# A hybrid attention and state-space block on one core: attention emitted in small pieces at fixed places, one softmax scaling moved into the head's norm, group norm one unit later

## Chip, cores, metric

One core of one Trainium2 chip. The metric is the device time of one execution, in microseconds (us). The kernel before takes 1214.12 us (median of three runs, 1212.49 to 1216.79).

## What is computed

One decoder block over 512 positions of width 1024, in float32:

```python
h = rms_norm(x, norm_mix_g);  proj = h @ w_in          # q, k, v, z, xbc, dt, gates
a = softmax(q1 k1 + bias) - lam * softmax(q2 k2 + bias)  # causal, 8 heads, two maps of 64 each
o = rms_norm(a @ v, attn_subln_g) * (1 - lam_init)      # per head, 128 wide
xbc = silu(causal_dwconv(xbc));  y = ssd_chunked_scan(...)   # 4 groups of 8 heads, chunks of 128
y = group rms_norm((y + xs * d_skip) * silu(z))
mixed = sigmoid(g_attn) * (y_attn @ w_proj_attn) + sigmoid(g_ssm) * (y_ssm @ w_proj_ssm)
x = x + mixed @ w_out
u = causal_dwconv(rms_norm(x) @ w_up);  x = x + (silu(u_gate) * u_val) @ w_down
```

## The kernel before

Every large product is made of three matmuls: each operand is split into a high part and a low remainder (xH, xL; weights wh, wl), and high*high, high*low and low*high are summed in PSUM. A c-tile (ctile) is 24 such matmuls of 512 columns for 128 output channels; a token block (in_block, L214) is four times 24 matmuls of 256 columns. Weights come in 179 units of 128x1024. `Weights.load` issues the DMA, casts to the high part on ScalarE (L83) and subtracts for the low part on VectorE or, for the numbers in `pool_units` (L75), on GpSimd (L86). Three raw buffers and four pairs of parts are kept, and a load is given a priority 600 instructions ahead of its place.

The program runs in this order:

- The norm of x, then dt and its cumulative sums, whose transposes (L267) go to TensorE.
- The state-space stage: 64 units in the hand-written order SSD_UNITS, each a convolved c-tile (B, C, x), a gate c-tile (z, e) or an output projection (p). `at` hangs steps of the chunked scan, and the transposes tokens_b and tokens_x (L325), behind unit numbers. SSD_AT gives for each group the units after which its chunks, its statistics (chunk_stat) and its group_norm are emitted. group_norm starts with the matmuls L483 that need the diagonal tile made by ScalarE at L474.
- Attention: for each of four head pairs att_in makes q, k and v in three token blocks and norms q and k. att_prep transposes them for one head, att_head runs four row blocks: logits (L654, L655), bias and row maximum on VectorE, exponentials on ScalarE, the second map scaled on ScalarE (L663), the difference on VectorE (L664). A queue `pending` holds each block's transposes (L610) back by AVLAG = 2 blocks and its products with v (L620) by one more; the fourth ends in the head's norm (L629 to L636) and finish (L642 to L646).
- Mix: per c-tile a gate c-tile, then the c-tile with yaH and yaL (the head outputs), then m, mH, mL.
- The output projection, the second norm, the feed-forward part.

The framework turns the emitted program into one queue for each engine. Emission order is the priority, and where its plan finds an instruction not ready in time, a later one goes ahead. So the matmuls of the next in_block lie partly between those of att_head. [...]

PSUM holds three c-tile accumulators (mm), two for transposes (tpp) and, in attention, two for logits (lgp) and one for the head's output (pop).

## Time and profile before

| | |
|---|---|
| median of three runs | 1214.12 us |
| the profiled execution | 1212.06 us |
| its span, first to last instruction | 1209.9 us |
| TensorE busy / VectorE / ScalarE / GpSimd | 1144.9 / 775.8 / 594.2 / 237.4 us |
| mean granted TensorE clock | 0.977 |

PE is the matmul engine, PEld its weight loads, DVE VectorE, ACT ScalarE, POOL GpSimd, SP SyncE with the DMA queue. L204 is line 204 of the kernel. [...] The matmul records overlap, so the pace of matmuls is read from counts over stretches and not from the length of one record.

### The profile page before, as it was taken

The page shows a single profiled execution, that of the slowest core. Times are in us where ns is not written, and L with a number is a line of the kernel's source. Part 1 is how long each engine was busy: PE and PEld are TensorE (multiplying, and loading weights), DVE is VectorE, ACT ScalarE, POOL GpSimd, SP SyncE. Part 2 cuts the span into 40 slices and gives each one's busy share as a digit, 9 for nine tenths or more (in the row PEclk, how much of TensorE's full clock was granted, in tenths as well). Part 3 has the DMA queues.
Part 4 walks back from the last instruction along what each step waited for, and adds up shares of the span by engine and source line. Part 5 has one row for each costly group of instructions (what it writes and reads, how often), then busy time and mean ns, then how long its engine had stood idle before and what let it go on. Part 6 is the DMA issues. An engine that isn't in the chain of part 4 may idle for free.

```text
span 1209.9 us, 15891 instructions
## 1 busy us (share of the span) xinstructions
PE 1144.9 (95%) x5934; PEld 960.8 (79%) x5934; DVE 775.8 (64%) x1312; ACT 594.2 (49%) x1154; POOL 237.4 (20%) x206
## 2 busy tenths in 40 slices
PE   5899997999999999998988988999999999999998
PEld 4688776887887889997978766887888888888887
DVE  7767768679876565468585875444777777773221
ACT  5674665665574232558484873233444444441210
POOL 2024334333433320451423000003000000000000
PEclk9899998999999999999898998999999999999999
DMA  6552332342433223221212112244232323323330
GB/s 221 91 134 93 119 100 80 124 118 90 133 109 96 70 87 117 72 75 44 71 42 73 53 36 70 90 136 135 75 105 90 102 90 103 101 92 115 112 105 18
DMA packets 56125, 114.47 MB, mean 95 GB/s; under 512 B 20640, under 2 KB 28496, under 8 KB 56048
## 3 DMA queue, kind: packets, MB, share of 16 engines
q1 hardware_dynamic: 56048, 113.45, 30.4%
q8 instruction: 47, 0.77, 0.3%
q14 instruction: 30, 0.25, 0.1%
HBM read 111.19 MB, written 2.24 MB: 94 GB/s over the span
## 4 chain that ended last, share of the span: by engine, by line
PE 78%; DVE 9%; ACT 8%; issue 3%; POOL 1%; DMA 1%; SPq 0%; POOLq 0%; ACTq 0%; DVEq 0%
PE mm L204 20%; PE mm L205 20%; PE mm L206 20%; PE mm L222 3%; PE mm L224 3%; PE mm L223 3%; DVE xc L318 1%; ACT wh L83 1%; DVE Bc L318 1%; PE sm L452 1%; PE po L620 1%; PE lg L654 1%; ACT dec L401 1%; ACT p L659 1%; PE sm L429 1%
## 5 line engine op out<-in xcount | busy, mean ns | idle before, releaser
L83 ACT CAST wh<-wr 128x1024 fp32r<-128x1024 f32 x179 | 187.4, 1048 | 253.0 <-PE mm L205 224.8
L86 DVE TENSOR_TENSOR wl<-wr,wh 128x1024 fp32r<-128x1024 f32 x130 | 160.2, 1233 | 101.9 <-ACT wh L83 100.6
L204 PE MATMUL mm<-xH,wh 128*128 128x512 f32 x456 | 184.1, 404 | 7.3 <-ACT xH L175 7.1
L206 PE MATMUL mm<-xH,wl 128*128 128x512 f32 x456 | 180.2, 395 | 0.7 <-DVE wl L86 0.7
L205 PE MATMUL mm<-xL,wh 128*128 128x512 f32 x456 | 180.2, 395 | 0.0
L86 POOL TENSOR_TENSOR wl<-wr,wh 128x1024 fp32r<-128x1024 f32 x49 | 118.4, 2426 | 151.5 <-ACT wh L83 125.4
L206 PE MATMUL mm<-hH,wl 128*128 128x512 f32 x352 | 137.7, 391 | 0.0
L204 PE MATMUL mm<-hH,wh 128*128 128x512 f32 x352 | 137.6, 391 | 0.0
L205 PE MATMUL mm<-hL,wh 128*128 128x512 f32 x352 | 137.6, 391 | 0.0
L222 PE MATMUL mm<-wh,xH 128*128 128x256 f32 x384 | 111.9, 291 | 5.1 <-ACT qksq L532 5.1
L223 PE MATMUL mm<-wl,xH 128*128 128x256 f32 x384 | 111.1, 289 | 0.0
L224 PE MATMUL mm<-wh,xL 128*128 128x256 f32 x384 | 110.7, 288 | 0.0
L204 PEld LDWEIGHTS mm<-xH,wh 128*128 128x128 f32 x456 | 86.9, 191 | 25.8 <-ACT xH L175 7.1
L206 PEld LDWEIGHTS mm<-xH,wl 128*128 128x128 f32 x456 | 86.6, 190 | 19.1 <-DVE wl L86 1.1
L205 PEld LDWEIGHTS mm<-xL,wh 128*128 128x128 f32 x456 | 86.8, 190 | 17.8 <-DVE xL L176 0.5
L222 PEld LDWEIGHTS mm<-wh,xH 128*128 128x128 f32 x384 | 75.8, 197 | 5.8 <-ACT qksq L532 5.7
L204 PEld LDWEIGHTS mm<-hH,wh 128*128 128x128 f32 x352 | 66.4, 189 | 13.9
L205 PEld LDWEIGHTS mm<-hL,wh 128*128 128x128 f32 x352 | 66.4, 189 | 13.9
L206 PEld LDWEIGHTS mm<-hH,wl 128*128 128x128 f32 x352 | 66.4, 189 | 13.7
L318 DVE SCALAR_TENSOR_TENSOR xc<-raw,pc,xc 128x512 f32<-128x512 f32 x48 | 64.9, 1353 | 18.9 <-ACT xc L316 18.1
L223 PEld LDWEIGHTS mm<-wl,xH 128*128 128x128 f32 x384 | 75.8, 197 | 0.2
L224 PEld LDWEIGHTS mm<-wh,xL 128*128 128x128 f32 x384 | 75.8, 197 | 0.1
(229 smaller groups left out, 2240.6 us busy)
## 6 DMA issues: line engine op xcount, KB each, us to landing
wr<-in_ws SPq DMA_DIRECT2D x179, 512.0 KB, 3.5
dec<-cum_d SPq DMA_DIRECT2D x16, 512.0 KB, 4.4
ec<-ecum_d SPq DMA_DIRECT2D x24, 128.0 KB, 3.7
...
```

The lines of the kernel that those rows point to most:

```text
L83: nc.scalar.copy(out=hi, in_=raw)
L86: eng.tensor_sub(out=lo, in0=raw, in1=hi.bitcast(F32))
L204: T.matmul(ps, lhsT=h, rhs=rH(k), start=(k == 0), stop=False)
L205: T.matmul(ps, lhsT=h, rhs=rL(k), start=False, stop=False)
L206: T.matmul(ps, lhsT=l, rhs=rH(k), start=False, stop=(k == n - 1))
L222: T.matmul(ps, lhsT=xH[k][:, sl], rhs=h, start=(k == 0), stop=False)
L223: T.matmul(ps, lhsT=xH[k][:, sl], rhs=l, start=False, stop=False)
L224: T.matmul(ps, lhsT=xL[k][:, sl], rhs=h, start=False, stop=(k == NK - 1))
L318: V.scalar_tensor_tensor(out=dst, in0=raw[:, j:j + S], scalar=w[j], in1=dst, op0=ALU.mult, op1=ALU.add)
L401: A.activation(out=dec[:, h], in_=dec[:, h], func=AF.Relu, scale=-1.0, bias=qcol[:, 0, c, g * HPG + h:g * HPG + h + 1])
L429: T.matmul(yo[:, j * P:(j + 1) * P], lhsT=state[:, j * P:(j + 1) * P], rhs=st["C"][:, cs], start=True, stop=True)
L452: T.matmul(yd[(h % 2) * 64:(h % 2) * 64 + 64, (h // 2) * P:(h // 2 + 1) * P], lhsT=xk[:, h * 64:(h + 1) * 64], rhs=dec[:, h], start=True, ...
```

## The change

- Attention is emitted piece by piece. block_pieces cuts a token block into eight pieces of 12 matmuls, gate_pieces a gate c-tile into four of 6, pa_pieces the first 7/8 of an attention projection into four. Lists give, for each head, the piece after which prep, logits, flip_a, values and head_out stand. A pair's steps lie between the pieces of the next pair and of one gate c-tile. The last pair's lie between five gate c-tiles and three unfinished attention projections. `pending`, `late` and AVLAG are gone; the eight gates have tiles of their own (gts).
- Softmax: the block is left scaled by its first map's sum. One small coefficient cf replaces the ScalarE pass L663, and the scale r is applied in the head's norm. For the first two row blocks both maps share one PSUM tile, one bias addition and one maximum.
- The norm of q and k is one chain of 32 columns in place of two of 16.
- group_norm of groups 0 to 2 stands one unit later; z1 stands ahead of p0, and x3 ahead of p3, in groups 2 and 3; the first tokens_b stands two units later and the first tokens_x one.
- The low parts of the 31 odd units 3 to 63 are made on VectorE in place of GpSimd; GpSimd makes those of units 71 to 90 (before: 71 to 88), among which there are now two gate units.
- The tile cb comes from another pool, rsqrt has other buffer counts, and an unused column is no longer computed.

```diff
-        o += [(n, g - 2 if n[0] == "p" else g) for n in "B z0 C p0 x0 p1 x1 p2 x2 p3 x3 z1 z2 z3".split()]
+        o += [(n, g - 2 if n[0] == "p" else g) for n in "B z0 C z1 p0 x0 p1 x1 p2 x2 x3 p3 z2 z3".split()]
...
-SSD_AT = [(11, (12, 14, 16, 18), (12, 15, 17, 19), 21, 22),
-          (22, (23, 25, 28, 31), (23, 26, 29, 32), 34, 35),
-          (35, (36, 38, 41, 44), (36, 39, 42, 45), 47, 48),
+SSD_AT = [(11, (12, 14, 16, 18), (12, 15, 17, 19), 21, 23),
+          (22, (23, 25, 28, 31), (23, 26, 29, 32), 34, 36),
+          (35, (36, 38, 41, 44), (36, 39, 42, 45), 47, 49),
           (47, (48, 50, 52, 54), (48, 51, 53, 55), 57, 58)]
...
-        self.pool_units = frozenset(range(3, 65, 2)) | frozenset(range(71, 89))
+        self.pool_units = frozenset(range(71, 91))
...
-        it = small.tile([P, 16], I32, name="rsi", bufs=3)[:, :n]
-        y = small.tile([P, 16], F32, name="rsy", bufs=3)[:, :n]
-        t = small.tile([P, 16], F32, name="rst", bufs=2)[:, :n]
+        it = small.tile([P, 32], I32, name="rsi", bufs=2)[:, :n]
+        y = small.tile([P, 32], F32, name="rsy", bufs=2)[:, :n]
+        t = small.tile([P, 32], F32, name="rst", bufs=4)[:, :n]
...
+            at.setdefault(n + (2 if n else 4), []).append(lambda: tokens_b(st))
...
-            at.setdefault(n + 2, []).append(lambda: tokens_x(g, j, xc))
+            at.setdefault(n + (3 if n < 4 else 2), []).append(lambda: tokens_x(g, j, xc))
...
-    def att_in():
-        st = {}
-        for nm in ("q", "k"):
-            raw = ap.tile([P, 4, 4, 64], F32, name="qk", bufs=4)
-            ss = small.tile([P, 16], F32, name="qkss", bufs=2)
-
-            def done(t, ps):
-                A.copy(out=raw[:, t].rearrange("p a d -> p (a d)"), in_=ps)
...
-            in_block(done)
-            v = small.tile([P, 16], F32, name="qkv", bufs=2)
-            V.tensor_scalar(out=v, in0=ss, scalar1=1.0 / 64, scalar2=1e-6, op0=ALU.mult, op1=ALU.add)
-            rr = small.tile([P, 16], F32, name="qkr", bufs=2)
-            rsqrt(v, rr, 16)
...
+    pairs = [{} for _ in range(4)]
...
+    def block_pieces(done):
+
+        u, hold = [], {}
+
+        def piece(t, half):
+            if not u:
+                u.extend(W.next() for _ in range(2))
+            if half == 0:
+                hold["ps"] = mm.tile([P, S], F32, name="mm")[:, :256]
+            ps = hold["ps"]
+            sl = slice(t * P, (t + 1) * P)
+            for k in range(4 * half, 4 * half + 4):
+                h, l = (w[:, (k % 4) * 256:(k % 4 + 1) * 256] for w in u[k // 4])
+                T.matmul(ps, lhsT=xH[k][:, sl], rhs=h, start=(k == 0), stop=False)
+                T.matmul(ps, lhsT=xH[k][:, sl], rhs=l, start=False, stop=False)
+                T.matmul(ps, lhsT=xL[k][:, sl], rhs=h, start=False, stop=(k == NK - 1))
+            if half == 1:
+                done(t, ps)
+        return [lambda t=t, half=half: piece(t, half) for t in range(4) for half in range(2)]
...
+    def gate_pieces(c):
...
+        def piece(i):
+            if i == 0:
+                hold["w"], hold["ps"] = W.next(), mm.tile([P, S], F32, name="mm")
+            (h, l), ps = hold["w"], hold["ps"]
+            for k in range(2 * i, 2 * i + 2):
+                hk, lk = h[:, k * P:(k + 1) * P], l[:, k * P:(k + 1) * P]
+                T.matmul(ps, lhsT=hk, rhs=xH[k], start=(k == 0), stop=False)
+                T.matmul(ps, lhsT=hk, rhs=xL[k], start=False, stop=False)
+                T.matmul(ps, lhsT=lk, rhs=xH[k], start=False, stop=(k == NK - 1))
+            if i == 3:
+                V.tensor_mul(out=gts[c], in0=ps, in1=r_bc)
+                A.activation(out=gts[c], in_=gts[c], func=AF.Tanh, scale=0.5)
...
+    def pair_pieces(p_):
...
+            A.copy(out=raw[:, t].rearrange("p a d -> p (a d)"), in_=ps)
+            sq = ap.tile([P, 4, 64], F32, name="qksq", bufs=1)
+            A.activation(out=sq.rearrange("p a d -> p (a d)"), in_=ps, func=AF.Square, scale=r_col[:, t:t + 1])
+            V.tensor_reduce(out=ss[:, i * 16 + t * 4:i * 16 + (t + 1) * 4], in_=sq, axis=AX.X, op=ALU.add)
+            if i == 1 and t == 3:
+                v = small.tile([P, 32], F32, name="qkv", bufs=2)
+                V.tensor_scalar(out=v, in0=ss, scalar1=1.0 / 64, scalar2=1e-6, op0=ALU.mult, op1=ALU.add)
+                rr = small.tile([P, 32], F32, name="qkr", bufs=2)
+                rsqrt(v, rr, 32)
+                for j, nm in enumerate("qk"):
+                    r1 = rr[:, j * 16:(j + 1) * 16]
+                    V.tensor_mul(out=r1.rearrange("p (t a) -> p t a", t=4), in0=r1.rearrange("p (t a) -> p t a", t=4),
+                                 in1=r_col.unsqueeze(2).to_broadcast([P, 4, 4]))
+                    w = st[nm].rearrange("p t a d -> p (t a) d")
+                    G.tensor_mul(out=w, in0=w, in1=r1.unsqueeze(2).to_broadcast([P, 16, 64]))
...
-    def att_prep(h, st):
-        hh = h % 2
-        qL = qlow[hh]
+    def prep(h):
+        st, hh, H = pairs[h // 2], h % 2, heads_[h]
...
-        qq, qL, ks, bias, vt = prep
+        H["bias"] = ap.tile([P, 256], F32, name="bias")
+        G.tensor_copy(out=H["bias"], in_=bass.AP(tensor=b0.tensor, offset=b0.offset + 255, ap=[list(b0.ap[0]), [-1, 256]]))
+        H["r"] = small.tile([P, 4, 2], F32, name="es", bufs=3)
...
+    def logits(h, i):
...
+        nm, ss = small.tile([P, 2], F32, name="nm", bufs=8), small.tile([P, 2], F32, name="sums", bufs=5)
+        if i < 2:
+            lg = lgp.tile([P, S], F32, name="lg")
+            lgs = [lg[:, m * n:(m + 1) * n] for m in range(2)]
+        else:
+            lgs = [lgp.tile([P, S], F32, name="lg")[:, :n] for _ in range(2)]
+        pr = []
+        for m in range(2):
+            T.matmul(lgs[m], lhsT=H["q"][m][:, i * P:(i + 1) * P], rhs=H["k"][m][:, :n], start=True, stop=False)
+            T.matmul(lgs[m], lhsT=qlow[hh][m][:, i * P:(i + 1) * P], rhs=H["k"][m][:, :n], start=False, stop=True)
+            if i >= 2:
+                V.tensor_add(out=lgs[m][:, n - nb:n], in0=lgs[m][:, n - nb:n], in1=bias)
+                V.tensor_reduce(out=nm[:, m:m + 1], in_=lgs[m], axis=AX.X, op=ALU.max, negate=True)
+        if i < 2:
+            both = lg[:, :2 * n].rearrange("p (m n) -> p m n", m=2)
+            V.tensor_add(out=both, in0=both, in1=bias.unsqueeze(1).to_broadcast([P, 2, n]))
+            V.tensor_reduce(out=nm, in_=both, axis=AX.X, op=ALU.max, negate=True)
+        for m in range(2):
+            p_ = ap.tile([P, S], F32, name="p", bufs=6)[:, :n]
+            A.activation(out=p_, in_=lgs[m], func=AF.Exp, bias=nm[:, m:m + 1], accum_out=ss[:, m:m + 1])
+            pr.append(p_)
+        V.reciprocal(out=H["r"][:, i], in_=ss)
+        cf = small.tile([P, 1], F32, name="cf", bufs=3)
+        V.scalar_tensor_tensor(out=cf, in0=H["r"][:, i, 1:2], scalar=nlam[:, 0:1], in1=ss[:, 0:1], op0=ALU.mult, op1=ALU.mult)
+        V.scalar_tensor_tensor(out=pr[0], in0=pr[1], scalar=cf[:, 0:1], in1=pr[0], op0=ALU.mult, op1=ALU.add)
+        H["a", i] = pr[0]
+
+    def flip_a(h, i):
+        H, n = heads_[h], (i + 1) * P
+        tp = tpp.tile([P, S], F32, name="tp")
+        for b in range(i + 1):
+            T.transpose(out=tp[:, b * P:(b + 1) * P], in_=H["a", i][:, b * P:(b + 1) * P], identity=ident)
+        aT = H["aT", i] = ap.tile([P, S], F32, name="aT")
+        A.copy(out=aT[:, :n], in_=tp[:, :n])
+
...
+                     start=(b == 0), stop=(b == i))
+        if i < 3:
+            return
+        o = H["o"] = ap.tile([P, 4, P], F32, name="o")
+        sq = ap.tile([P, P], F32, name="qksq", bufs=1)
+        v = small.tile([P, 4], F32, name="ov", bufs=3)
+        A.copy(out=o.rearrange("p a d -> p (a d)"), in_=po)
+        for t in range(4):
+            A.activation(out=sq, in_=o[:, t], func=AF.Square, scale=H["r"][:, t, 0:1], accum_out=v[:, t:t + 1])
+        V.tensor_scalar(out=v, in0=v, scalar1=1.0 / P, scalar2=1e-5, op0=ALU.mult, op1=ALU.add)
+        rr = small.tile([P, 4], F32, name="orr", bufs=2)
+        rsqrt(v, rr, 4)
+        V.scalar_tensor_tensor(out=rr, in0=rr, scalar=1.0 - LAM_INIT, in1=H["r"][:, :, 0], op0=ALU.mult, op1=ALU.mult)
+        G.tensor_mul(out=o, in0=o, in1=rr.unsqueeze(2).to_broadcast([P, 4, P]))
...
+    def head_out(h):
...
+    def pa_pieces(c):
...
+        def piece(i):
...
+                hold["w"], hold["ps"] = W.next(), mm.tile([P, S], F32, name="mm")
+                pas.append((hold["w"], hold["ps"]))
+            (h, l), ps = hold["w"], hold["ps"]
+            for k in range(2 * i, min(2 * i + 2, NH - 1)):
+                hk, lk = h[:, k * P:(k + 1) * P], l[:, k * P:(k + 1) * P]
+                T.matmul(ps, lhsT=hk, rhs=yaH[k], start=(k == 0), stop=False)
+                T.matmul(ps, lhsT=hk, rhs=yaL[k], start=False, stop=False)
+                T.matmul(ps, lhsT=lk, rhs=yaH[k], start=False, stop=False)
+        return [lambda i=i: piece(i) for i in range(4)]
...
-    st = att_in()
-    prep = att_prep(0, st)
+
+    pieces, start, todo = pair_pieces(0), [], {}
     for p_ in range(4):
-        prep = att_head(2 * p_, prep, lambda: att_prep(2 * p_ + 1, st))
-        st = att_in() if p_ < 3 else None
-        prep = att_head(2 * p_ + 1, prep, lambda: att_prep(2 * p_ + 2, st) if p_ < 3 else None)
-    drain(0)
-    while late:
-        late.pop(0)()
-        drain(0)
+        start.append(len(pieces))
+        if p_ < 3:
+            pieces += pair_pieces(p_ + 1) + gate_pieces(p_)
+        else:
+            for c in range(3, 8):
+                pieces += gate_pieces(c)
+            pa = [pa_pieces(c) for c in range(3)]
+            pieces += [f for q in pa for f in q[:3]] + [q[3] for q in pa]
+
+    def put(n, f, *a):
+        todo.setdefault(n, []).append(lambda: f(*a))
+
+    put(start[0] - 3, prep, 0)
+    for p_ in range(4):
+        for e, (prep_at, ats) in enumerate(zip((5, 22), ((0, 3, 7, 10), (14, 17, 21, 24)) if p_ < 3 else ((0, 3, 6, 9), (12, 15, 18, 21)))):
+            h = 2 * p_ + e
+            if h < NH - 1:
+                put(start[p_] + prep_at, prep, h + 1)
+            for i, n in enumerate(ats):
+                n += start[p_]
+                lag = 7 if p_ < 3 else 6
+                put(n, logits, h, i)
+                put(n + lag, flip_a, h, i)
+                put(n + lag + 2, values, h, i)
+            put(ats[3] + start[p_] + lag + 7, head_out, h)
+    for n, f in enumerate(pieces):
+        f()
+        for g in todo.pop(n, []):
+            g()
+    for n in sorted(todo):
+        for g in todo[n]:
+            g()
...
-    if True:
-        for c in range(8):
-            ps = in_ctile()
...
-            h, l = W.next()
-            pa = ctile(lambda k: (h[:, k * P:(k + 1) * P], l[:, k * P:(k + 1) * P]), NK,
-                       lambda k: yaH[k], lambda k: yaL[k])
...
+    for c in range(8):
+        (h, l), pa = pas[c] if c < 3 else (W.next(), mm.tile([P, S], F32, name="mm"))
+        for k in range(NH - 1 if c < 3 else 0, NH):
+            hk, lk = h[:, k * P:(k + 1) * P], l[:, k * P:(k + 1) * P]
+            T.matmul(pa, lhsT=hk, rhs=yaH[k], start=(k == 0), stop=False)
+            T.matmul(pa, lhsT=hk, rhs=yaL[k], start=False, stop=False)
+            T.matmul(pa, lhsT=lk, rhs=yaH[k], start=False, stop=(k == NH - 1))
+        m = gts[c]
+        V.scalar_tensor_tensor(out=m, in0=m, scalar=1.0, in1=pa, op0=ALU.add, op1=ALU.mult)
```

## Rows read from the trace of the kernel before

**Rows 1.** The page's first line of figures: busy time and share of each engine.
```profile
PE 1144.9 (95%) x5934; PEld 960.8 (79%) x5934; DVE 775.8 (64%) x1312; ACT 594.2 (49%) x1154; POOL 237.4 (20%) x206
```

**Rows 2.** The page's chain that ended last, by engine.
```profile
PE 78%; DVE 9%; ACT 8%; issue 3%; POOL 1%; DMA 1%; SPq 0%; POOLq 0%; ACTq 0%; DVEq 0%
```

**Rows 3.** Windows: length, busy us (count) of PE, PEld, DVE, ACT, POOL; clock, DMA.
```profile
33.00:62.00 29.00, 23.19 (x94) 17.84 (x94) 19.86 (x29) 19.50 (x35) 2.78 (x3) 0.82 0.55 80
170.00:196.00 26.00, 17.09 (x86) 12.99 (x85) 18.33 (x32) 14.41 (x33) 12.00 (x9) 0.80 0.27 89
268.00:286.00 18.00, 16.21 (x75) 12.80 (x74) 16.31 (x31) 9.24 (x16) 2.60 (x3) 1.00 0.28 88
362.00:376.00 14.00, 11.61 (x53) 8.32 (x52) 10.90 (x22) 5.17 (x10) 4.40 (x3) 0.88 0.35 114
...
33.00:466.35 433.35, 412.54 (x2061) 334.85 (x2060) 312.46 (x418) 237.70 (x499) 142.20 (x103) 0.97 0.35 103
500.90:739.00 238.10, 211.34 (x1452) 190.37 (x1451) 163.75 (x482) 159.99 (x407) 60.32 (x36) 0.94 0.18 54
...
571.60:583.00 11.40, 7.21 (x39) 7.02 (x39) 7.76 (x25) 9.50 (x22) 1.91 (x3) 0.70 0.05 12
633.20:645.00 11.80, 7.14 (x41) 6.76 (x40) 7.80 (x25) 9.13 (x17) 3.46 (x3) 0.71 0.05 13
718.00:739.00 21.00, 12.62 (x44) 9.04 (x43) 8.04 (x29) 8.04 (x17) 2.08 (x2) 0.68 0.07 25
739.00:798.60 59.60, 59.60 (x264) 49.35 (x263) 30.61 (x37) 18.26 (x24) 0.00 (x0) 1.00 0.34 106
```

**Rows 4.** Windows laid on the stretches at the lower clock, same columns.
```profile
42.70:53.00 10.30, 7.40 (x25) 5.17 (x26) 7.87 (x14) 4.94 (x10) 0.75 (x2) 0.50 0.51 151
182.60:193.00 10.40, 4.99 (x16) 3.48 (x16) 8.02 (x20) 4.83 (x9) 2.56 (x3) 0.51 0.18 54
370.00:374.00 4.00, 4.00 (x17) 2.85 (x17) 2.26 (x4) 2.05 (x5) 1.06 (x1) 0.57 0.32 126
575.20:582.00 6.80, 5.67 (x26) 5.67 (x27) 5.46 (x19) 4.93 (x10) 0.65 (x1) 0.50 0.00 1
636.60:643.50 6.90, 5.08 (x22) 4.89 (x23) 4.59 (x12) 4.86 (x8) 1.56 (x2) 0.51 0.00 0
722.00:739.00 17.00, 11.15 (x34) 8.08 (x35) 5.03 (x18) 6.01 (x14) 1.47 (x2) 0.60 0.07 26
```

**Rows 5.** Waits of PE: releaser, us in total, times, longest us.
```profile
PE tp L483 <- ACT t L474: 12.2, 3, 8.1
PE lg L654 <- ACT p L659: 2.2, 5, 0.8
```

**Rows 6.** Timeline of PE at the first transposes: start, length, line, tiles.
```profile
45.60 0.48 PE L325 MATMUL mm<-ident,Bc 128*128 128x128 f32 x1 [5.81 <-DVE Bc L320]
46.01 0.55 PE L267 MATMUL sm<-ident,cum 32*128 32x32 f32 x2
```

**Rows 7.** Timeline of VectorE from 271.59 us.
```profile
271.59 0.17 DVE L118 TENSOR_SCALAR rsi<-ssv 128x4 int32<-128x4 int32 x1
271.80 2.38 DVE L119 TENSOR_SCALAR rsy<-rsi 128x4 int32<-128x4 int32 x1
```

**Rows 8.** Timeline of GpSimd, the same moment.
```profile
271.75 2.40 POOL L86 TENSOR_TENSOR wl<-wr,wh 128x1024 fp32r<-128x1024 f32 x1 [6.33 <-ACT wh L83]
```

**Rows 9.** Groups of VectorE, 33 to 466 us: count, busy, mean ns, idle.
```profile
L86 DVE TENSOR_TENSOR wl<-wr,wh 128x1024 fp32r<-128x1024 f32 x33 | 41.4, 1254 | 18.3 <-ACT wh L83 18.2
```

**Rows 10.** Line L663: durations in ns, minimum/median/maximum, first and last start.
```profile
L663 ACT ACTIVATE p<-p,es x32: 389/562/726, 510.3 to 719.0; 128x128 f32<-128x128 f32 x8, 128x256 f32<-128x256 f32 x8, 128x384 f32<-128x384 f32 x8, 128x512 f32<-128x512 f32 x8
```

**Rows 11.** A window on the densest attention stretch, same columns.
```profile
559.00:576.00 17.00, 11.62 (x81) 9.91 (x81) 14.22 (x45) 13.87 (x42) 1.44 (x2) 0.98 0.04 9
```

**Rows 12.** Timeline of PE at the end of attention.
```profile
725.40 1.91 PE L620 MATMUL po<-vt,aT 128*128 128x128 f32 x8
...
733.57 1.11 PE L642 MATMUL tp<-ident,o 128*128 128x128 f32 x4 [4.59 <-POOL o L636]
735.46 1.22 PE L204 MATMUL mm<-yaH,wh 128*128 128x512 f32 x2 [0.78 <-ACT yaH L644]
```

More of the change, by code (lines that the diff above doesn't have):

```diff
@@ L28 @@
 NEG = -1.0e30
-AVLAG, PREP_AT = 2, 3
 LAM_INIT = 0.8 - 0.6 * math.exp(-0.3 * 0)
@@ L156, in block_kernel @@
     r_col = fixed.tile([P, 4], F32, name="r_col")
-    rh_col = fixed.tile([P, 4], F32, name="rh_col")
     r_bc = const.tile([P, S], F32, name="r_bc")
@@ L212, in in_ctile @@
                      lambda k: xH[k], lambda k: xL[k])
-    def in_block(done):
-        u = [W.next() for _ in range(2)]
-        for t in range(4):
-            ps = mm.tile([P, S], F32, name="mm")[:, :256]
-            for k in range(NK):
-                h, l = (w[:, (k % 4) * 256:(k % 4 + 1) * 256] for w in u[k // 4])
-                sl = slice(t * P, (t + 1) * P)
-                T.matmul(ps, lhsT=xH[k][:, sl], rhs=h, start=(k == 0), stop=False)
-                T.matmul(ps, lhsT=xH[k][:, sl], rhs=l, start=False, stop=False)
-                T.matmul(ps, lhsT=xL[k][:, sl], rhs=h, start=False, stop=(k == NK - 1))
-            done(t, ps)
     qcol = const.tile([P, 3, NCH, 32], F32, name="qcol")
@@ L271, in block_kernel @@
     acc = [accp.tile([P, S], F32, name=f"acc{c}") for c in range(8)]
-    c01 = fixed.tile([P, 2], F32, name="c01")
+    nlam = fixed.tile([P, 16], F32, name="nlam")[:, 0:1]
     gqk = const.tile([P, 1], F32, name="gqk")
@@ L552, in block_kernel @@
-    pending, late = [], []
-    def drain(n):
-        while len(pending) > n:
-            f = pending.pop(0)
-            ready = late[:]
-            late.clear()
-            f()
-            for r in ready:
-                r()
+    pairs = [{} for _ in range(4)]
+    heads_ = [{} for _ in range(NH)]
+    def block_pieces(done):
[15 more added lines that the diff above has]
+        return [lambda t=t, half=half: piece(t, half) for t in range(4) for half in range(2)]
@@ new lines, in pair_pieces, with done, vdone @@
+    def pair_pieces(p_):
+        st = pairs[p_]
+        def done(i, t, ps):
+            if i == 0 and t == 0:
+                st["ss"] = small.tile([P, 32], F32, name="qkss", bufs=2)
+            if t == 0:
+                st["qk"[i]] = ap.tile([P, 4, 4, 64], F32, name="qk", bufs=4)
+            ss, raw = st["ss"], st["qk"[i]]
+            A.copy(out=raw[:, t].rearrange("p a d -> p (a d)"), in_=ps)
[13 more added lines that the diff above has]
+                    G.tensor_mul(out=w, in0=w, in1=r1.unsqueeze(2).to_broadcast([P, 16, 64]))
+        def vdone(t, ps):
+            if t == 0:
+                st["v"] = ap.tile([P, 4, 256], F32, name="vt")
+            A.activation(out=st["v"][:, t], in_=ps, func=AF.Copy, scale=r_col[:, t:t + 1])
+        return (block_pieces(lambda t, ps: done(0, t, ps)) + block_pieces(lambda t, ps: done(1, t, ps))
+                + block_pieces(vdone))
@@ L593, in att_prep @@
                                    op0=ALU.mult, op1=ALU.subtract)
-            ks.append(k2)
+            H["k"].append(k2)
         b0 = ap.tile([P, 256], F32, name="b0", bufs=1)
         nc.sync.dma_start(out=b0, in_=bass.AP(tensor=line_d.tensor, offset=line_d.offset + 384 * h, ap=[[1, P], [1, 256]]))
-        bias = ap.tile([P, 256], F32, name="bias")
-        G.tensor_copy(out=bias, in_=bass.AP(tensor=b0.tensor, offset=b0.offset + 255, ap=[list(b0.ap[0]), [-1, 256]]))
-        return qq, qL, ks, bias, st["v"]
@@ new lines, in flip_a, with values @@
+    def flip_a(h, i):
[5 more added lines that the diff above has]
+        A.copy(out=aT[:, :n], in_=tp[:, :n])
+    def values(h, i):
+        H, hh, vt = heads_[h], h % 2, pairs[h // 2]["v"]
+        if i == 0:
+            H["po"] = pop.tile([P, S], F32, name="po")
+        po, aT = H["po"], H["aT", i]
+        for b in range(i + 1):
+            T.matmul(po[:, i * P:(i + 1) * P], lhsT=aT[:, b * P:(b + 1) * P], rhs=vt[:, b, hh * P:(hh + 1) * P],
+                     start=(b == 0), stop=(b == i))
[12 more added lines that the diff above has]
+        G.tensor_mul(out=o, in0=o, in1=rr.unsqueeze(2).to_broadcast([P, 4, P]))
@@ new lines, in head_out @@
+    def head_out(h):
+        tp = tpp.tile([P, S], F32, name="tp")
+        for t in range(4):
+            T.transpose(out=tp[:, t * P:(t + 1) * P], in_=heads_[h]["o"][:, t], identity=ident)
+        sg = pc[:, C_SG:C_SG + 1]
+        A.activation(out=yaH[h], in_=tp, func=AF.Copy, scale=sg)
+        V.scalar_tensor_tensor(out=yaL[h], in0=tp, scalar=sg, in1=yaH[h].bitcast(F32),
+                               op0=ALU.mult, op1=ALU.subtract)
+    pas = []
+    def pa_pieces(c):
+        hold = {}
+        def piece(i):
+            if i == 0:
+                hold["w"], hold["ps"] = W.next(), mm.tile([P, S], F32, name="mm")
[6 more added lines that the diff above has]
+                T.matmul(ps, lhsT=lk, rhs=yaH[k], start=False, stop=False)
+        return [lambda i=i: piece(i) for i in range(4)]
@@ L830 @@
         order += [q_[2 * p_:2 * p_ + 2], k_[2 * p_:2 * p_ + 2], v_[2 * p_:2 * p_ + 2]]
-    for c in range(8):
-        order += [gate[c:c + 1], pa[c:c + 1]]
+        if p_ > 0:
+            order.append(gate[p_ - 1:p_])
+    order += [gate[3:8], pa]
     order.append(wo)
```

108 lines of the change are left out of this document (15 added, 93 removed).

## Prediction

> **What bounds the kernel.** I read the page first. TensorE is busy 95% of the span [rows 1] and makes up 78% of the chain that ended last [rows 2], so what a change can give is TensorE's idle time and its time at the lower clock; the matmuls themselves stay. I then laid windows over the stages [rows 3]. In the state-space stage, 33 to 466 us, TensorE is busy 412.5 of 433.4 us: 20.8 us idle. In attention after its first three token blocks, 500.9 to 739 us, it is busy 211.3 of 238.1: 26.8 us idle. Other rows of that table show where the idle time sits. Windows set on the stretches at the lower clock [rows 4] say how much of them was work; at half speed half of that work's time is lost. In the state-space stage these are 7.4, 5.0 and 4.0 us of work (the last at 0.57, so 3.4 us at the lower level): 3.7 + 2.5 + 1.7 = 7.9 us. In attention 5.7 and 5.1 us at two places give 5.4 us, and in the tail about 8 of 11.2 us, because a mean of 0.60 over 17 us is 13.6 us at the lower level, part of it idle: 4 us. So 28.7 us are lost in the state-space stage and 36.2 in attention, 65 together. Last I asked whom TensorE waits for [rows 5] and opened the timelines there [rows 6 to 8, 12]. In each of the lower-clock stretches the clock fell during or just after an idle gap, which is why I count it with the gap.
>
> **Group norm one unit later, about 13.5 us.** L483 waits for ScalarE's diagonal tile three times, 12.2 us in all, 8.1 the longest [rows 5]. The unit that now goes ahead is 24 matmuls; a stretch of such matmuls alone holds 264 in 59.6 us [rows 3], 0.226 us each, so 5.4 us. That covers 5.4 of the 8.1 and all of the other two (4.1 us): 9.5. The lower clock that followed gives back up to 2.5 + 1.7 = 4.2 [rows 4]. Sum 13.7, and I take 13.5, with 6 below (the first wait stays long enough for the clock to fall) and 16.4 above (all of the wait and the clock). The projection p0 that follows the norm has its x-tile behind it as before, so nothing new is late but p0 itself.
>
> **First transposes later, about 4 us.** The first L325 waits 5.8 us for Bc [rows 6], and the lower clock after it costs 3.7. Two more units now lie ahead of it. But the very next rows are L267, the transposes of dt's cumulative sums, which VectorE delivers at about the same time. If they keep their place, TensorE stops there in place of L325. The bounds are 0 and 9.5; between them I take 4, since a unit is 5.4 us and some of it will lie ahead of L267.
>
> **Low parts from GpSimd to VectorE, 0.** 31 subtractions at 1.25 us [rows 9] put 39 us more on VectorE, which is busy 312 of 433 us [rows 3]: 351, or 85% of the shorter stage. Against it stands what GpSimd's subtraction does to VectorE: an operation on 4 columns took 2.38 us where its neighbour took 0.17 [rows 7], and a GpSimd subtraction ran over just that time [rows 8]. 2.2 us for each of 31 would be 68 us, none would be 0. So VectorE's time changes by something between +39 and -29 us. I take no effect on TensorE, because the cover is VectorE's idle 28%, with 0 to 17 us of cost in the range if that cover is gone (rival 3). [...]
>
> **Attention spread out, about 14 us.** Before, two heads' steps come in bursts. In the densest, 559 to 576 us, VectorE works 14.2 and ScalarE 13.9 of 17 us while TensorE works 11.6 [rows 11]. Over the whole stage they are busy only 69 and 67% (163.8 and 160.0 of 238.1) [rows 3]. So the work fits and its crowding is what costs. Two bursts end in the windows 571.6 to 583 and 633.2 to 645, with 4.2 and 4.7 us idle [rows 3] and 5.4 us lost to the clock: 14.3 us. With a piece of 12 matmuls between steps, and seven pieces between logits and their transposes, I take 13 of it (bounds 7 and 14.3). The rest of the idle time outside the tail is 26.8 - 8.9 - 8.4 = 9.5 us in many small waits. I take 2 us for each of four pairs to remain, a gain of 1.5 (bounds 9.5 and a loss of 10: 5 us a pair, half the idle share of the two windows above).
>
> **L663 and the merged operations, 0 by themselves.** 32 passes at 0.56 us [rows 10] take 18 us off ScalarE and 0.4 to 0.7 us off each block's chain. They run beside TensorE, and what they free is part of the 13 above. The shared bias addition and maximum and the single chain for the norm of q and k shorten VectorE likewise. The eight gate c-tiles move, with their weight loads, into attention; their 192 matmuls cost the same there. GpSimd's two more subtractions lie beside idle GpSimd (60 of 238 us busy [rows 3]).
>
> **The tail, about 3.5 us.** After the last product with v, TensorE cannot finish any projection until the last head is normed. From the end of L620, 725.40 + 1.91, to the first matmul with the new yaH at 735.46 [rows 12] is 8.15 us. In the new order only two short pieces of three matmuls lie there, 1.4 us, since three unfinished projections hold all three accumulators. So about 6.8 us stay idle, and I add 2 for the clock: 8.8 against 8.4 + 4 = 12.4 us [rows 3, 4]. Gain 3.6; the bounds are 1 and 8.
>
> **Sum.** 13.5 + 4 + 0 + 13 + 1.5 + 0 + 3.6 = 35.6 us. I take off 1.5 for more changes between kinds of matmul, which no row prices (bounds 0 and 5): 34. From the profiled 1212.1 us that is 1178; the median stands 2.1 us above the profiled time, which would give 1180. I predict 1179.
>
> **Rivals.**
> 1. The attention stage gives nothing: q and k are normed only seven pieces ahead of prep, GpSimd's queue holds weight subtractions of 2.4 us [rows 8], and the waits go to prep and the tail. For it: GpSimd's norm of the head is the last wait of all [rows 12]. Against: no burst is left. 1179 + 16.6 = 1196.
> 2. All waits vanish but the tail's 8.8 us: 65 - 8.8 = 56, so 1156 to 1158. For it: both VectorE and ScalarE are a third idle over the stage. Against: L267, and queues that no longer have slack by reordering.
> 3. VectorE is too full in the state-space stage: accumulators are freed late, and the stage gains nothing. 1179 + 17 = 1196. For it: 85% load; against: no wait on an accumulator is among the large ones now.
> 4. Slower. The plan used to slip matmuls of the next block into the gaps; a fixed place takes that freedom, and every one of the 112 attention steps (14 a head) can stop the queue. The nearest row is a logits matmul waiting for its PSUM buffer, 2.2 us in five waits, 0.44 us each [rows 5]. At that price 112 steps cost 49 us in place of the 8 above: 1179 + 41 = 1220. It decides against the change from (33 + 8) / 112 = 0.37 us a step. Against it: the steps it needs stand five to seven pieces, 8 to 11 us, behind their sources. [...]
>
> **Chances and range.** The forecast (both stages gain, 1165 to 1190) 0.52; rival 1 0.13; rival 3 0.12; rival 2 0.11; rival 4 0.08; no change, gains and losses equal, 0.04. What a measurement of this kernel can tell from no change is about 0.3%, 3.6 us. Faster is 0.52 + 0.13 + 0.12 + 0.11 = 0.88, same 0.04, slower 0.08. The range takes in rivals 1 and 3 with the bounds of the split's cost, up to 1201, and reaches down to 1160; outside are rival 2 in most of its cases, rival 4 and no change, about 0.2.
>
> **What would show it.** Right: waits of L483 under 3 us in all; a clock of 1.00 from 62 to 466 us; no gap of over 2 us between the first token block and the last product with v; one gap of 6 to 7 us before the projections, with the lower clock behind it. The norm is wrong if L483 still waits over 5 us; the first transposes, if L267 heads the waits; the spread, if small waits at L654, L610, L620 or L576 sum to over 20 us; the split, if matmuls wait for L314 or L365. The forecast fails if TensorE's idle time in attention does not fall under 20 us.

## The result, and the profile after

The changed kernel takes 1175.82 us (median of 4 runs, 1175.06 to 1176.51) against 1214.44 us of the kernel before on the same chip: a ratio of 0.968, 95% interval 0.966 to 0.970. It is faster by 38.6 us, where 34 were forecast, and the time lies inside the range. That the total came out well is luck: errors of opposite sign cancelled. The state-space stage with all that goes with it gave 27.0 us where 17.5 were forecast, attention 12.1 where 16.6 were, and within the stage the time came from another edit than the forecast said.

In the changed kernel the group norm's matmuls L483 are L466, the transposes L325 are L308, L267 is L251, the products with v L620 are L663, flip_a's transposes L610 are L653, those of head_out L642 are L682, the state's matmuls L429 are L412, the weight subtraction L86 is L85, and the softmax difference L664 is L646.

The first lines of the page and of its chain, answering to [rows 1, 2]:

```profile
PE 1130.8 (96%) x5934; PEld 956.2 (81%) x5934; DVE 770.5 (66%) x1259; ACT 579.2 (49%) x1122; POOL 166.5 (14%) x177
...
PE 87%; DVE 7%; ACT 3%; issue 2%; POOL 1%; DMA 0%; SPq 0%; ACTq 0%; POOLq 0%; DVEq 0%
```

TensorE makes up 87% of the chain in place of 78. GpSimd lost 71 us of work, and VectorE, which took 31 subtractions over, is not busier: 770.5 us against 775.8. That is a first sign of how much GpSimd's subtractions had stretched VectorE's work.

Windows on the changed kernel: the state-space stage, attention with the mix up to the first matmul of the output projection, attention after its first three token blocks, and three of the six stretches at the lower clock (columns as in [rows 3]):

```profile
30.70:444.20 413.50, 406.42 (x2055) 331.13 (x2054) 307.15 (x447) 235.16 (x498) 71.97 (x74) 0.99 0.37 108
444.20:764.80 320.60, 296.89 (x2002) 273.07 (x2001) 210.73 (x475) 178.52 (x424) 74.69 (x44) 0.96 0.23 70
...
478.70:737.30 258.60, 236.71 (x1611) 218.09 (x1610) 177.18 (x422) 155.22 (x385) 65.25 (x38) 0.95 0.20 60
...
177.50:187.70 10.20, 7.26 (x20) 5.89 (x21) 10.20 (x14) 5.04 (x11) 3.95 (x5) 0.50 0.32 103
532.50:539.30 6.80, 5.88 (x17) 4.83 (x18) 4.67 (x7) 3.72 (x9) 0.84 (x2) 0.50 0.45 141
...
730.40:737.30 6.90, 4.62 (x12) 3.44 (x13) 2.18 (x5) 2.50 (x3) 1.04 (x1) 0.51 0.01 2
```

Attention with the mix has the same matmuls in both kernels, so it needs its window on the kernel before too:

```profile
466.35:798.60 332.25, 305.49 (x2001) 274.27 (x2000) 209.30 (x557) 191.74 (x455) 69.94 (x42) 0.96 0.22 68
```

The granted clock reads 1.00 or 0.50 all through the traces of the two kernels; a mean like 0.96 comes of windows that hold both. In the changed kernel matmuls of 512 columns start 0.43 us apart at 0.50 (at 535.16 and 535.59 us) and 0.23 us apart at 1.00 (at 188.00 and 188.23 us), so of such work's time a little under half was lost where the prediction took half.

The state-space stage is 19.9 us shorter (433.35 in [rows 3], 413.50 now): its idle time fell from 20.8 to 7.1 us. Attention with the mix is 11.7 us shorter, but its idle time fell only from 26.8 to 23.7 us. The other 8.6 us are busy time, at the same mean clock of 0.96. VectorE fills its stretch at 177.5 us: 10.20 of 10.20 us.

Whom TensorE waits for in the changed kernel, answering to [rows 5]:

```profile
PE tp L682 <- DVE ql L601: 8.2, 3, 3.6
...
PE tp L682 <- POOL o L677: 6.7, 3, 5.3
PE tp L653 <- DVE ql L601: 6.3, 4, 2.8
PE sm L412 <- ACT state L422: 3.1, 1, 3.1
...
PE mm L308 <- DVE Bc L303: 0.7, 1, 0.7
```

The wait of the group norm on its diagonal tile (12.2 us) is gone and the first transposes wait 0.7 in place of 5.8. New are 14.5 us of waits of L682 and L653 for L601, the low part of q that prep makes. A timeline of all engines at the first of them, and at the tail, answering to [rows 12]:

```profile
527.94 5.01 POOL L85 TENSOR_TENSOR wl<-wr,wh 128x1024 fp32r<-128x1024 f32 x2
528.10 2.65 DVE L646 SCALAR_TENSOR_TENSOR p<-p,cf 128x384 f32<-128x384 f32 x1
...
529.43 0.39 PE L538 MATMUL mm<-xH,wh 128*128 128x512 f32 x1
530.67 0.67 DVE L601 TENSOR_TENSOR ql<-tp,qq 64x512 fp32r<-64x512 f32 x1
...
532.58 0.69 DVE L601 TENSOR_TENSOR ql<-tp,qq 64x512 fp32r<-64x512 f32 x1 [0.90 <-ACT qq L600]
...
533.42 1.09 PE L682 MATMUL tp<-ident,o 128*128 128x128 f32 x4 [3.61 <-DVE ql L601]
...
731.91 1.12 PE L682 MATMUL tp<-ident,o 128*128 128x128 f32 x4 [5.32 <-POOL o L677]
...
733.80 1.22 PE L756 MATMUL mm<-yaH,wh 128*128 128x512 f32 x2 [0.78 <-ACT yaH L684]
```

prep holds both transpose buffers until L601 and its neighbours have read them, and head_out needs one. L601 is late because L646 ahead of it on VectorE takes 2.65 us: it began at 528.10, just after the first of the two GpSimd subtractions (527.94 to 530.33), and ended 0.4 us behind it. With no GpSimd subtraction the same L646 takes 0.60 us (below). The 3.61 us gap and the lower clock (0.50) from 532.5 us follow. The tail stands as forecast: 5.32 + 0.78 us idle.

### The profile page after: what moved, and what is told of

Its sections match the earlier page's. It is cut to its first block, busy times and chain, and to the rows that moved or that the text cites. A ratio compares the mean times of both kernels' runs of the same rounds, so it can differ in the third digit from the quotient of the medians.

```text
span 1174.7 us, 15747 instructions
## 1 busy us (share of the span) xinstructions
PE 1130.8 (96%) x5934; PEld 956.2 (81%) x5934; DVE 770.5 (66%) x1259; ACT 579.2 (49%) x1122; POOL 166.5 (14%) x177
## 4 chain that ended last, share of the span: by engine, by line
PE 87%; DVE 7%; ACT 3%; issue 2%; POOL 1%; DMA 0%; SPq 0%; ACTq 0%; POOLq 0%; DVEq 0%
PE mm L201 20%; PE mm L202 20%; PE mm L203 20%; PE mm L524 4%; PE mm L522 4%; PE mm L523 4%; PE po L663 1%; DVE wl L85 1%; PE sm L435 1%; PE mm L539 1%; PE mm L540 1%; PE mm L538 1%; PE mm L756 1%; PE mm L757 1%; PE mm L758 1%
## 5 line engine op out<-in xcount | busy, mean ns | idle before, releaser
L85 DVE TENSOR_TENSOR wl<-wr,wh 128x1024 fp32r<-128x1024 f32 x159 | 196.7, 1238 | 106.7 <-ACT wh L82 105.1
L201 PE MATMUL mm<-xH,wh 128*128 128x512 f32 x392 | 159.2, 406 | 7.8 <-ACT xH L173 7.2
L202 PE MATMUL mm<-xL,wh 128*128 128x512 f32 x392 | 154.9, 395 | 0.0
L203 PE MATMUL mm<-xH,wl 128*128 128x512 f32 x392 | 154.7, 395 | 0.0
L201 PEld LDWEIGHTS mm<-xH,wh 128*128 128x128 f32 x392 | 74.6, 190 | 24.1 <-ACT xH L173 7.2
L202 PEld LDWEIGHTS mm<-xL,wh 128*128 128x128 f32 x392 | 74.6, 190 | 16.0 <-DVE xL L174 1.0
L203 PEld LDWEIGHTS mm<-xH,wl 128*128 128x128 f32 x392 | 74.4, 190 | 16.3 <-DVE wl L85 0.3
L202 PEld LDWEIGHTS mm<-hL,wh 128*128 128x128 f32 x352 | 66.1, 188 | 13.8
L203 PEld LDWEIGHTS mm<-hH,wl 128*128 128x128 f32 x352 | 66.1, 188 | 13.5
L201 PE MATMUL mm<-aH,wh 128*128 128x512 f32 x176 | 68.5, 389 | 0.0
L202 PE MATMUL mm<-aL,wh 128*128 128x512 f32 x176 | 68.5, 389 | 0.0
```

Of the source, the lines that this page charges most:

```text
L85: eng.tensor_sub(out=lo, in0=raw, in1=hi.bitcast(F32))
L201: T.matmul(ps, lhsT=h, rhs=rH(k), start=(k == 0), stop=False)
L202: T.matmul(ps, lhsT=h, rhs=rL(k), start=False, stop=False)
L203: T.matmul(ps, lhsT=l, rhs=rH(k), start=False, stop=(k == n - 1))
```

## The experiments

Twelve kernels were run; the kernel before took 1214.2 to 1214.9 us (median) beside them.

| kernel | median, us | range | ratio to before, 95% |
|---|---|---|---|
| splits_alone | 1196.34 | 1194.03 to 1196.69 | 0.984 to 0.987 |
| places_alone | 1208.35 | 1207.53 to 1210.07 | 0.994 to 0.997 |
| state_space_half | 1187.89 | 1187.28 to 1189.07 | 0.977 to 0.980 |
| changed_old_splits | 1196.68 | 1194.48 to 1197.85 | 0.984 to 0.987 |
| changed_idle_gpsimd_reads | 1197.18 | 1195.63 to 1197.60 | 0.985 to 0.987 |
| changed_idle_gpsimd_writes | 1176.32 | 1174.38 to 1177.34 | 0.967 to 0.970 |
| changed_early_tokens | 1181.41 | 1178.50 to 1183.63 | 0.970 to 0.974 |
| changed_early_norm | 1177.38 | 1175.22 to 1178.31 | 0.968 to 0.971 |
| changed_scaled_on_act | 1178.84 | 1178.15 to 1180.12 | 0.970 to 0.972 |
| changed_no_gpsimd_split | 1162.02 | 1160.28 to 1163.53 | 0.955 to 0.959 |
| old_attention_no_gpsimd_split | 1184.16 | 1183.10 to 1184.37 | 0.974 to 0.977 |
| no_split_last_head_earlier | 1154.77 | 1154.35 to 1157.19 | 0.950 to 0.953 |

### Which part of the state-space stage gave the time

splits_alone is the kernel before with one line of the change, places_alone the kernel before with the units' order, SSD_AT and the token transposes of the change, state_space_half both, changed_old_splits the changed kernel with the 31 odd units back on GpSimd:

```diff
-        self.pool_units = frozenset(range(3, 65, 2)) | frozenset(range(71, 89))
+        self.pool_units = frozenset(range(71, 89))
```

> The kernel before with one edit: the low parts of the 31 odd units of the state-space stage are made on VectorE in place of GpSimd. Theory 'places': what the state-space stage gained came from where tokens_b, tokens_x and group_norm stand; the splits gave only the 2.3 us by which the first norm ended earlier. It expects -1 to -4 us (ratio 0.997 to 0.999) and L483 and L325 still waiting over 10 us together. Rival 'ports': freeing VectorE from GpSimd's subtractions shortened the chains that L483 and L325 wait for; it expects -8 to -15 us (ratio 0.988 to 0.993) and L483 under 6 us in all.

> The kernel before with the state-space places of the change alone: tokens_b and tokens_x of the start later, group_norm one unit later with the new unit order; the splits stay on GpSimd. 'Places' expects -18 to -22 us (ratio 0.982 to 0.985). 'Ports' expects -8 to -13 us (0.989 to 0.993), with 3 us or more of the wait of L483 left.

> Both edits in the kernel before, attention untouched. If the two stages are independent this stands 20 to 24 us under the kernel before (ratio 0.980 to 0.984), and attention's rewrite is worth the other 12 to 14 us. If the attention stage's gain had come from the better start that the state-space stage gives it, this kernel would already be near the changed kernel, 0.972 or less.

> The changed kernel with the 31 odd units' low parts back on GpSimd (units 71 to 90 as changed). 'Places' expects +1 to +4 us against the changed kernel (1177 to 1180 us); 'ports' expects +8 to +15 us (1184 to 1191).

The one line is worth 18.6 us on the kernel before, more than either theory gave it. The places alone are worth 6.6. Both together give 27.0, and the old line in the changed kernel costs 20.9. So the attention half, from state_space_half to the changed kernel, is worth 12.1.

How the line acts is read from the waits in splits_alone and from its window on the stage, to be held against [rows 3, 5, 6]:

```profile
PE tp L483 <- ACT t L474: 4.1, 1, 4.1
PE mm L325 <- DVE Bc L320: 3.6, 1, 3.6
...
30.30:450.10 419.80, 409.90 (x2054) 332.59 (x2054) 306.36 (x447) 236.59 (x498) 73.70 (x74) 0.98 0.36 106
```

The very waits that the places were to remove fell from 12.2 and 5.8 us, with every step at its old place. The two make up 10.3 of the 18.6 us. The stage as a whole is 13.6 us shorter (419.80 us in place of 433.35) and begins 2.7 us sooner (at 30.30 in place of 33.00). In places_alone the two waits vanish or halve, but others come:

```profile
PE mm L204 <- ACT xtok L339: 5.2, 1, 5.2
...
PE sm L429 <- ACT state L439: 3.1, 1, 3.1
PE mm L325 <- DVE Bc L320: 3.0, 1, 3.0
...
PE sm L267 <- DVE cum L252: 2.3, 1, 2.3
```

### Is it GpSimd's reading, its queue, or the late low part?

Three causes were left for the 20.9 us: GpSimd's subtraction blocks VectorE; it fills GpSimd's queue, so that chunk operations come late; or the low part itself comes late from GpSimd. Both kernels are the changed one, with work added on GpSimd that no other engine waits for (the added lines are shortened here):

```diff
             eng.tensor_sub(out=lo, in0=raw, in1=hi.bitcast(F32))
+            # reads, odd units 3 to 63:
+            nc.gpsimd.tensor_sub(out=scr, in0=hi[:, :960], in1=hi[:, :960])
+            # writes, in its place:
+            nc.gpsimd.tensor_copy(out=scr[:, :1], in_=hi[:, :1])
+            nc.gpsimd.memset(scr, 0.0); nc.gpsimd.memset(scr, 1.0)
```

> The changed kernel, and in addition GpSimd subtracts the high part of each of the 31 odd weight units 3 to 63 from itself, 960 columns, into a tile that nobody reads, when that high part is there. VectorE, ScalarE, TensorE and the DMAs do the same work as in the changed kernel, and no instruction but GpSimd's own waits for the extra ones. Theory one, GpSimd's reading of SBUF blocks VectorE's operations: each of the 31 lasts about 2.3 us, VectorE's operations beside them are stretched by some 25 to 40 us in the state-space stage, and most of what the moved splits gained is given back: 1187 to 1197 against 1176. Theory two, the splits gained because the low part comes sooner from VectorE (1.25 us in place of 2.4, and not behind GpSimd's chunk work): nothing waits for the extra instructions, 1175 to 1178. Theory three, GpSimd's own queue was too full and its chunk operations came late: also 1187 to 1197, but then the kernel with writes in place of reads gives the same.

> As the kernel with the idle subtractions, but GpSimd copies one column of the high part and then sets the unused tile of 960 columns twice, about 2 us in all by its memset of 512 columns (0.52 us): it is as busy as with the subtraction, but it only writes. Theory one, it is GpSimd's reading that blocks VectorE's operations with two inputs: little is blocked, 1175 to 1180. If writing blocks as well, at least the operations with one input, 1182 to 1195, and VectorE's stretched time shows which. Theory three, GpSimd's queue: the same as with the subtractions, 1187 to 1197. Theory two: 1175 to 1178 in both.

Reads cost 21.4 us, writes 0.5. The lines for the reads: the window from 0 to 478 us (columns as in [rows 3]), a convolution step of VectorE, and GpSimd's idle subtractions:

```profile
0.00:478.00 478.00, 445.93 (x2219) 361.34 (x2220) 367.97 (x496) 254.98 (x528) 158.33 (x115) 0.98 0.36 111
...
L301 DVE SCALAR_TENSOR_TENSOR xc<-raw,pc,xc 128x512 f32<-128x512 f32 x48 | 52.8, 1100 | 2.5 <-ACT xc L299 1.9
...
L85 POOL TENSOR_TENSOR scr<-wh 128x960 f32<-128x960 f32 x31 | 78.7, 2539 | 130.7 <-ACT wh L82 130.7
```

The same for the writes:

```profile
0.00:478.00 478.00, 461.19 (x2405) 379.96 (x2406) 343.12 (x518) 264.26 (x544) 163.00 (x180) 0.99 0.38 115
...
L301 DVE SCALAR_TENSOR_TENSOR xc<-raw,pc,xc 128x512 f32<-128x512 f32 x48 | 42.5, 885 | 2.5 <-ACT xc L299 1.9
...
L85 POOL MEMSET scr<- 128x960 f32 x62 | 55.9, 902 | 3.4
```

And the changed and the earlier kernel, whose L318 is this L301:

```profile
0.00:478.00 478.00, 461.37 (x2410) 380.24 (x2410) 343.11 (x518) 265.56 (x547) 84.28 (x88) 0.99 0.38 115
...
L301 DVE SCALAR_TENSOR_TENSOR xc<-raw,pc,xc 128x512 f32<-128x512 f32 x48 | 42.4, 884 | 2.7 <-ACT xc L299 2.1
```

```profile
L318 DVE SCALAR_TENSOR_TENSOR xc<-raw,pc,xc 128x512 f32<-128x512 f32 x48 | 64.9, 1353 | 18.9 <-ACT xc L316 18.1
```

GpSimd is busy 158 us in one and 163 in the other, so its queue is not the cause. The low part comes from VectorE in both, so it is not that either. What differs is VectorE. The convolution step takes 884 ns in the changed kernel, 885 beside writes, 1100 beside idle reads and 1353 in the kernel before, beside GpSimd's real subtractions. This step lies on the chain to L325 and to every chunk. With reads VectorE is also busy 24.9 us longer in the same 478 us (368.0 against 343.1) for fewer instructions. TensorE is idle 32.1 us of them in place of 16.6, and the waits that grew are for VectorE's results:

```profile
PE sm L435 <- DVE dec L391: 4.6, 2, 3.3
PE mm L202 <- DVE yL L471: 3.7, 3, 2.4
PE mm L308 <- DVE Bc L303: 3.2, 1, 3.2
```

Theory one holds. That the weight buffers came free later, since the idle subtraction reads the high part, is not it: in that trace no instruction of another engine waits for the idle subtractions.

A timeline of the kernel with writes shows the two kinds side by side:

```profile
23.48 1.22 DVE L85 TENSOR_TENSOR wl<-wr,wh 128x1024 fp32r<-128x1024 f32 x1
23.57 1.86 POOL L85 MEMSET scr<- 128x960 f32 x2
24.61 0.85 DVE L117 TENSOR_SCALAR rsi<-rsv 128x4 int32<-128x4 int32 x1
...
101.94 1.86 POOL L85 MEMSET scr<- 128x960 f32 x2
...
103.02 0.74 DVE L301 SCALAR_TENSOR_TENSOR xc<-raw,pc,xc 128x512 f32<-128x512 f32 x1
...
103.77 1.06 POOL L424 TENSOR_TENSOR state<-state,etot 128x512 f32<-128x512 f32 x1
103.88 1.50 DVE L301 SCALAR_TENSOR_TENSOR xc<-raw,pc,xc 128x512 f32<-128x512 f32 x1
```

Beside the memsets a VectorE operation with two inputs kept its time: 1.22 us for L85, whose mean in the changed kernel is 1.24, and 0.74 for L301 at 103.02, whose median there is 0.75. Beside GpSimd's reading L424 the same L301 took 1.50. A one-input operation on 4 columns, L117, did stop for the memset: it took 0.85 us, where it takes 0.16 in the changed kernel, and it ended at 25.46 us, the memsets at 25.43. So in these runs the two-input operations were stretched beside GpSimd's reads and not beside its writes, and L117 was held to the end of the memset; how it was held is not shown.

### The places, one at a time

Each is the changed kernel with one place put back: the token transposes, or the group norm with the units' order.

```diff
-            at.setdefault(n + (2 if n else 4), []).append(lambda: tokens_b(st))
+            at.setdefault(n + 2, []).append(lambda: tokens_b(st))
...
-SSD_AT = [(11, (12, 14, 16, 18), (12, 15, 17, 19), 21, 23),
+SSD_AT = [(11, (12, 14, 16, 18), (12, 15, 17, 19), 21, 22),
```

> The changed kernel with the first tokens_b and tokens_x two units behind their source again. With the splits on VectorE the places together were worth 6 to 8 us (1196.3 against 1187.9). Theory 'ports' expects +2 to +5 us here (1178 to 1181 us), the wait at the transposes of Bc being about 3.6 us as in the run with the splits alone. The reading by milestones, in which the first transposes gave 9.7 us, expects +8 to +10 us (1184 to 1186).

> The changed kernel with group_norm and the unit order of groups 2 and 3 as before. 'Ports' expects +1 to +5 us (1177 to 1181), since with the splits on VectorE the norm's matmuls waited 4.1 us once. The prediction's own term for this step, 13.5 us, would give 1189.

The transposes' place is worth 5.6 us, and early again they wait 3.6 us for Bc, as the first theory said:

```profile
PE mm L308 <- DVE Bc L303: 3.6, 1, 3.6
```

The group norm's is worth 1.6, which the ranges of the runs do not tell from nothing. With the norm early again one wait on the diagonal tile comes back, and the wait of L412, which the late norm had brought, is gone (3.1 us in the changed kernel):

```profile
PE tp L466 <- ACT t L457: 6.0, 1, 6.0
```

### Attention

changed_scaled_on_act gives the second map's scaling back to ScalarE:

```diff
-        V.scalar_tensor_tensor(out=pr[0], in0=pr[1], scalar=cf[:, 0:1], in1=pr[0], op0=ALU.mult, op1=ALU.add)
+        A.activation(out=pr[1], in_=pr[1], func=AF.Copy, scale=cf[:, 0:1])
+        V.tensor_add(out=pr[0], in0=pr[1], in1=pr[0])
```

> The changed kernel with the second map scaled again by a pass on ScalarE (32 passes, about 18 us of ScalarE in all) and then added on VectorE, all places unchanged. If the pass runs beside TensorE as the prediction says, 0 to +3 us (1176 to 1179). If ScalarE's crowding sets the waits at the preparation of the heads, +6 us or more (1182 and up), and the gaps before the transposes of heads 1, 3 and 5 grow by about the length of a pass, 0.7 us each, or more.

It costs 3.0 us, the upper end of the first reading and half of what the second asked for. Where the 3.0 us go is not shown: the waits for L601 are no longer in all than in the changed kernel (14.4 us against 14.5), and in the profiled execution attention with the mix is 1.3 us longer.

changed_no_gpsimd_split and old_attention_no_gpsimd_split take GpSimd's last subtractions, those of attention, away too, from the changed kernel and from state_space_half:

```diff
-        self.pool_units = frozenset(range(71, 91))
+        self.pool_units = frozenset()
```

> The changed kernel with no unit split on GpSimd: units 71 to 90 go to VectorE too. VectorE gets 20 subtractions of 1.24 us, 25 us, in an attention stage of about 240 us in which it is 65 to 70% busy, and is no longer held up behind GpSimd's subtractions (19 us in the changed kernel's attention by its trace). 'Ports' expects -3 to -9 us (1167 to 1173), with the gaps at heads 1, 3 and 5 shorter. If VectorE's load is what counts, +2 to +8 us (1178 to 1184).

> The kernel before with the changed state-space stage (1188 before), and with the low parts of units 71 to 88 on VectorE too, so that GpSimd makes none. It tells what the new attention is worth when no GpSimd subtraction is in it: this time less 1162. Theory one, the blocking costs the old attention as much as the new one (15.9 us of stretched VectorE time in the old, 19.0 in the new): 1174 to 1180, and the new attention is worth some 12 to 17. Rival, the old plan slips matmuls of the next block into the gaps and so hid the blocking: 1185 to 1190, and the new attention is worth about 25 once its own blocking is gone.

20 subtractions moved in the changed kernel give 13.8 us; 18 moved under the old attention give 3.7. So the new attention is worth 12.1 us with GpSimd's subtractions beside it and 22.1 without. The second expectation's rival came nearer. That the old plan hid the blocking because other matmuls could go ahead in it, where fixed places stop, is its explanation; the runs show the sizes, 3.7 against 13.8, and not the way. In changed_no_gpsimd_split the waits of the heads shrink, and so does L646 (2.65 us above):

```profile
PE tp L682 <- DVE ql L601: 2.9, 3, 1.0
PE tp L653 <- DVE ql L601: 1.8, 4, 0.6
```

```profile
527.81 0.60 DVE L646 SCALAR_TENSOR_TENSOR p<-p,cf 128x384 f32<-128x384 f32 x1
...
444.40:750.50 306.10, 290.97 (x2002) 266.88 (x2001) 213.91 (x495) 180.09 (x424) 27.54 (x24) 0.98 0.23 73
```

The last kernel goes on from there and tests the tail, where changed_no_gpsimd_split still has this gap:

```profile
716.57 1.11 PE L682 MATMUL tp<-ident,o 128*128 128x128 f32 x4 [5.33 <-POOL o L677]
```

```diff
-        for e, (prep_at, ats) in enumerate(zip((5, 22), ((0, 3, 7, 10), (14, 17, 21, 24)) if p_ < 3 else ((0, 3, 6, 9), (12, 15, 18, 21)))):
+        for e, (prep_at, ats) in enumerate(zip((5 - p_ // 3, 22), ((0, 3, 7, 10), (14, 17, 21, 24)) if p_ < 3 else ((0, 3, 6, 9), (10, 13, 15, 18)))):
```

> The changed kernel without any GpSimd split (1162 before), with the last head's four blocks two to three pieces earlier (after pieces 10, 13, 15, 18 in place of 12, 15, 18, 21) and its prep one piece earlier. 21 matmuls, 4.75 us, then lie between its last product with v and head_out, in place of 6, 1.4 us. If the tail's idle 5.3 us and the lower clock behind it are what is left there: the gap falls to about 2 us and the clock may hold, 1155 to 1159. Rival, the steps of the last head now come too soon after one another and TensorE stops at its logits or transposes instead: 1160 to 1165, with new waits at L653 or L630.

```profile
713.42 0.66 PE L682 MATMUL tp<-ident,o 128*128 128x128 f32 x4 [1.92 <-POOL o L677]
...
714.85 1.65 PE L756 MATMUL mm<-yaH,wh 128*128 128x512 f32 x3 [0.78 <-ACT yaH L684]
...
444.60:745.60 301.00, 289.52 (x2002) 265.65 (x2001) 213.60 (x495) 180.30 (x424) 27.50 (x24) 0.99 0.24 75
```

The gap fell from 5.33 to 1.92 us and the time by 7.25: 3.4 of these from the gap. The stretch at the lower clock there (means of 0.51 and 0.50) is 3.4 us long in place of 10.2 and holds 2.95 us of work in place of 6.75; half of the difference, 1.9 us, is what that gives by an estimate like the prediction's. The remaining 2 us are not accounted for. At 1154.77 us this version beats both kernels.

## Why the prediction was right in sum and wrong in its parts

**Low parts from GpSimd to VectorE, 0: the step that failed.** It measured 18.6 us alone and 20.9 in the whole. The bounds on VectorE's time were sound: with 29 instructions more, VectorE worked 307.2 us in place of 312.5 in the stage, so each subtraction moved cost 1.25 us and freed a little more. What failed is "no effect on TensorE, because the cover is VectorE's idle 28%". That cover is an average. The blocked operations lay in chains that TensorE waits for at their end, so what they lost showed at L483 (12.2 us of waits, 4.1 in splits_alone) and at L325 (5.8 and 3.6). [rows 7, 8] showed the blocking, and it was booked as VectorE's load, not as delay of the chain. The moved subtractions did not hold up GpSimd's chunk operations where it can be read: L455 takes 1490 ns on average before and 1513 in splits_alone, L433 1599 and 1543.

**Group norm, 13.5: too large.** The wait did go, as forecast, but two thirds of it was the blocking's: 12.2 us fell to 4.1 with the splits alone. What the place added was partly paid back by the new wait of L412 (3.1 us), and the lower clock (0.50) stayed at 177.5 us. Measured last, it is worth 1.6.

**First transposes, 4: about right,** 5.6. That L267 would take the wait over was true only with GpSimd's subtractions (2.3 us in places_alone). Both places together: 6.6 alone and 8.4 on top of the splits, against 17.5.

**Attention and tail, 13 + 1.5 + 3.6 - 1.5 = 16.6: 12.1, for other reasons.** This step failed too: it put the gain on idle time, of which only 3.1 us went (26.8 to 23.7). The bursts went, but waits for L601 took their place, and the forecast's own sign of failure came: TensorE's idle time was 258.6 - 236.7 = 21.9 us. "No gap over 2 us" was wrong: L682 waited 3.6 and L653 2.8 us at the longest. The stretches at the lower clock (0.50) add up to 27.3 us in attention in both kernels (four of 6.8 before; three of 6.8 and two of 3.4 now). The rest of the gain came from matmul time: 8.6 us less busy time for the same matmuls. The 1.5 us taken off for changes between kinds of matmul were the author's estimate: no row and no run shows such a cost, and in its place the runs showed these 8.6 us less. Worked out from the starts in the traces, where the granted clock was 1.00, TensorE's busy time from the start of a matmul to the start of whatever matmul stands next is 98 ns on average in place of 117 for a product with v, 79 in place of 98 for a transpose of flip_a, and 177 in place of 224 for the first of the two logits matmuls of a map. What made these times shorter was not tested and stays open.

**L663 and the merged operations, 0:** the scaling pass is worth 3.0 us. Back on ScalarE, its 32 passes take 18.0 us; the forecast had folded what they cost into the 13. The merged operations were not tested by themselves.

**The tail** was right in place and size: 5.32 + 0.78 us idle against a forecast 6.8, with the lower clock behind it (a mean of 0.51 from 730.4 to 737.3 us). Its gain of 3.6 was not measured by itself.

**Rivals.** Both stages gained, which speaks against rivals 1 and 3 as a whole; VectorE is too full only in one stretch, 177.5 to 187.7 us. Of rival 1, the part on GpSimd's queue was true in another way: its weight subtractions delayed VectorE (L646 took 2.65 us beside them and 0.60 without). Rival 2, that all waits but the tail's vanish, was kept off by the waits for L601. Rival 4's stops at every step did not come.

**Two bounds** do not follow from the numbers beside them: rivals 1 and 3 give 1196 each, not the 1201 at which the range ends, and 5 us for each pair is not half the idle share of the two windows: 0.37 and 0.39 of them were idle, and half of that is about 11 of a pair's 60 us. Neither touched the outcome.
